# One-hots for the expert weights from one 16-bit compare, a shorter lead over U, and 18 gathered rows moved beside the last build

## The chip, the cores and the metric

The kernel runs on one core of a Trainium2 chip. A core has five engines with a queue of instructions each: TensorE (PE in the profile; its weight loads are PEld), VectorE (DVE), ScalarE (ACT), GpSimd (POOL) and SyncE (SP). They work side by side and wait for each other by semaphores; 16 DMA engines move data for all of them. The metric is the device time of one execution in microseconds (us), lower is better.

## The reference, cut to what matters

The kernel computes one encoder layer on 512 tokens of width 1024: layer norm, two kinds of attention, layer norm, then a feed-forward part that picks experts for each token, a gate, and a last layer norm. The change lies in the feed-forward part alone:

```python
q = (xb @ w_q).reshape(PEER_CHUNK, PEER_HEADS, PEER_KEY_DIM)
s1 = jnp.einsum('thd,kd->thk', q[..., :half], sub_keys[0])
s2 = jnp.einsum('thd,kd->thk', q[..., half:], sub_keys[1])
v1, i1 = lax.top_k(s1, PEER_TOPK)
v2, i2 = lax.top_k(s2, PEER_TOPK)
cand = (v1[..., :, None] + v2[..., None, :]).reshape(...)
cv, ci = lax.top_k(cand, PEER_TOPK)
e1 = jnp.take_along_axis(i1, ci // PEER_TOPK, axis=-1)
e2 = jnp.take_along_axis(i2, ci % PEER_TOPK, axis=-1)
idx = (e1 * PEER_N_KEYS + e2).reshape(...)
g = jax.nn.softmax(cv, axis=-1)
u = u_table[idx]
hpre = jnp.einsum('td,ted->te', xb, u)
act = g * jax.nn.gelu(hpre, approximate=False)
return jnp.einsum('te,ted->td', act, v_table[idx])
```

Each token has 8 heads with 16 picks, so 128 of 16,384 experts. An expert is a pair of keys (e1, e2), each 0 to 127; it has a row of U and a row of V of 1024 float32 each.

## The kernel before

**Two ways to the experts.** The 512 tokens are four chunks of 128. Chunk 0 is gathered: for each of its 128 picks an indirect DMA of POOL fetches one row of U per token (128 rows of 4 KB), and VectorE takes the dot product with the token (gather_u, L1257; the fetch is fetch_u, L1251); later the same for V (gather_v, L1266). Chunks 1 to 3 (384 tokens) are done densely: all experts are taken in 128 blocks of 128, TensorE multiplies block i of U with the tokens, ScalarE applies Gelu (the tile ge), the result is multiplied by a matrix G of weights per expert and token, and a second product adds it, times block i of V, into PSUM (acc). Of the 384, the 96 of chunk 1 with the lowest numbers take no part in the product with U; own_rows (L1002) gathers their rows of U, in 96 groups of 128 rows, and puts the result into their weights.

**G is built by TensorE.** For a token, G is the sum over its 128 picks of two one-hot vectors' product: oh_i, 1 at the first key, and oh_j, the weight at the second key. build_g (L933) takes 8 tokens (OT) at a time, 16 groups to a chunk. In a group, VectorE writes the first `first` of eight one-hots oh_i by one compare (L974), ScalarE the others by Abs and Relu (L978, L979); VectorE writes eight oh_j, one tensor_scalar each (L987: equal, then times weight). TensorE multiplies the pairs (L953, one group behind), ScalarE copies the sums out of PSUM (L964) and every second group sends 1 MB to g_dram (L966). `first` is OV_OWN = 2 for chunks 2 and 3, built first, and OV = 5 for chunk 1, built last.

**The lead.** Beside the routing of the chunks (route, L840, nearly all VectorE) and the builds, TensorE works through the gate (192 matmuls of width 512, in 16 steps of 12) and through the first LEAD = 73 blocks of U (lead_block, L1059): eight float32 matmuls of width 288 for a block, straight from the loaded block. Of these the first SPILL = 56 results go to DRAM (ge_dram) and are read back later; the others stay on the chip. A half of the gate (512 columns) ends on VectorE and ScalarE (gate_end, L1100): four loads into the tile pl, issued together on SP, and for each of the four chunks an instruction of VectorE (L1116) that reads pl. The 55 blocks left are done in the stream (expert_in, L747) as 24 matmuls each: block and tokens are split into a high and a low part, ScalarE writes the high part, VectorE the low.

**Who sets the order.** From L1191 on the order on every engine is the order in which the Python code issues. The generators yield an estimate of the VectorE time that they just issued; run (L1173) and run_pe (L924) then issue as much work of TensorE as PACE times that amount (AHEAD and LAG shift it). own_rows is woven in likewise: each yield earns it a share OWN = 0.98 of VectorE time. A row group lands in one of four buffers (whi and wlo of the pool wst, two each); its fetch waits until VectorE has read the group four before it. VectorE, ScalarE and TensorE work through their queues in order.

**The stages.** Route of chunk 1; route of chunk 2, its build, route of chunk 3, its build, with own_rows woven into these; route of chunk 0; build of chunk 1; the rest of the lead, beside which the stream is prepared (L1300 to L1318: seven row fetches of chunk 0, the load of G, loads and splits of V, seven more rows; PRE = 14 in all). Then the stream of 128 steps: each takes a block of V, 18 matmuls into acc, as long as there are any a block of U (24 matmuls), and its part of the 257 gather steps by L1366.

## Time and profile before

| | us |
|---|---|
| median of 3 runs | 1578.45 |
| the three runs | 1568.41, 1578.45, 1581.92 |
| the profiled execution | 1574.03 |
| its span, first to last instruction | 1572.2 |
| first matmul of the lead | 416.2 |
| last product of the last build | 816.6 |
| first matmul of the stream | 845.8 |

The profile is of one execution. A group line has the source line, engine, operation, tiles written <- read with their shape, the count, then the busy time of all, the mean duration of one in ns, and the engine's idle time ahead of them with what ended it. Matmuls are pipelined: their durations overlap, and a step's cost is read from the distance of starts. A float32 matmul stands as two records. A stretch line has the stretch, its length, each engine's busy time with its number of instructions, the granted TensorE clock (1.00 is full), the mean busy share of the 16 DMA engines and GB/s; the share can exceed 1 a little.

### The profile page before, as it was taken

To read this page: it belongs to the slowest core of one execution; us is meant where nothing else is said; L and a number is where in the kernel's file an instruction comes from. 1 tells how busy PE (TensorE), PEld (TensorE's weight loads), DVE (VectorE), ACT (ScalarE), POOL (GpSimd) and SP (SyncE) were. 2 spreads that over 40 slices of the span, in tenths; PEclk is the share of its full clock that TensorE was granted. 3 is DMA by queue.
4 is the path that set the end of the run, shared out by engine and by line. 5 is a ranking of instruction groups with operands and counts; after the bars stand their busy time and mean duration, and the time that the engine had idled before them with its cause. 6 is when DMAs were issued, how large, how long until landed. Compare 5 with 4: busy or idle time off the path is not lost.

```text
span 1572.2 us, 23352 instructions
## 1 busy us (share of the span) xinstructions
PE 1534.2 (98%) x7963; PEld 1275.3 (81%) x7963; DVE 1311.6 (83%) x2989; ACT 690.2 (44%) x1269; POOL 490.9 (31%) x496
## 2 busy tenths in 40 slices
PE   8999899999999999999998999999999999999997
PEld 5788777788878887888886898898998878787785
DVE  7376795679899999889985798988989898899897
ACT  3365685333224672575562334334343433333333
POOL 1013100010024233432105455555555544344410
PEclk9999999999999999999999999999999999999999
DMA  6342340152369999999769999999999999999972
GB/s 224 97 114 80 89 121 28 54 151 81 104 211 346 343 368 352 371 418 363 248 235 394 375 382 374 383 378 355 373 378 338 359 360 382 384 379 387 379 281 81
DMA packets 204571, 437.21 MB, mean 278 GB/s; under 512 B 16770, under 2 KB 110370, under 8 KB 201380
## 3 DMA queue, kind: packets, MB, share of 16 engines
q1 hardware_dynamic: 138592, 210.27, 38.9%
q0 software_dynamic: 53984, 191.97, 33.0%
q10 hardware_dynamic: 11876, 33.49, 5.5%
q8 instruction: 63, 1.03, 0.3%
q14 instruction: 56, 0.46, 0.1%
...
## 4 chain that ended last, share of the span: by engine, by line
PE 68%; DVE 12%; DMA 11%; issue 4%; ACT 2%; SPq 1%; POOL 1%; ACTq 0%; POOLq 0%; DVEq 0%
PE mm L1069 9%; DMA v_raw<-in_v_rows_dram 8%; PE acc L104 6%; PE acc L105 6%; PE acc L106 6%; PE tr L953 5%; PE hp L104 4%; PE hp L106 3%; PE hp L105 3%; PE mm L104 3%; PE mm L106 3%; PE pj L104 3%; PE mm L105 3%; PE pj L105 3%; PE pj L106 3%
## 5 line engine op out<-in xcount | busy, mean ns | idle before, releaser
L1268 POOL DMA_INDIRECT gat<-in_v_rows_dram,i_sel x128 | 170.2, 1329 | 204.8 <-DVE base L1270 180.2
L1253 POOL DMA_INDIRECT gat<-in_u_rows_dram,i_sel x128 | 170.9, 1335 | 181.7 <-DVE scr L1259 123.9
L104 PE MATMUL acc<-v_hi,a_hi 128*128 128x512 f32 x552 | 216.5, 393 | 4.0 <-ACT a_hi L89 4.0
L106 PE MATMUL acc<-v_hi,a_lo 128*128 128x512 f32 x552 | 216.2, 392 | 0.2 <-DVE a_lo L90 0.2
L105 PE MATMUL acc<-v_lo,a_hi 128*128 128x512 f32 x552 | 215.6, 391 | 0.0
L90 DVE TENSOR_TENSOR wlo<-raw,whi 128x1024 fp32r<-128x1024 f32 (+3 forms) x134 | 156.9, 1172 | 65.9 <-ACT whi L89 65.3
L89 ACT CAST whi<-raw 128x1024 fp32r<-128x1024 f32 (+3 forms) x134 | 135.1, 1009 | 139.7 <-PE mm L105 40.3
L89 ACT CAST v_hi<-v_raw 128x1024 fp32r<-128x1024 f32 x92 | 96.6, 1050 | 209.4 <-issue 121.0
L1270 DVE SCALAR_TENSOR_TENSOR base<-gat,hdot,base 128x1024 f32<-128x1024 f32 x128 | 163.8, 1280 | 1.7
L1259 DVE SCALAR_TENSOR_TENSOR scr<-gat,h 128x1024 f32<-128x1024 f32 x128 | 156.6, 1223 | 2.9
L1069 PE MATMUL mm<-whole,raw 128*128 128x288 f32 x624 | 157.2, 406 | 0.3 <-DMA raw<-in_uT_dram 0.3
L1069 PE MATMUL hp<-whole,raw 128*128 128x288 f32 x544 | 138.8, 410 | 4.2 <-DMA raw<-in_uT_dram 4.2
L89 ACT CAST a_hi<-gt 128x384 fp32r<-128x384 f32 x126 | 64.6, 513 | 177.4 <-DVE gt L1353 133.2
L1069 PEld LDWEIGHTS mm<-whole,raw 128*128 128x128 f32 x624 | 116.0, 190 | 29.9 <-DVE ci L782 0.7
L90 DVE TENSOR_TENSOR v_lo<-v_raw,v_hi 128x1024 fp32r<-128x1024 f32 x92 | 112.6, 1223 | 26.9 <-ACT v_hi L89 26.6
L104 PE MATMUL hp<-hTh,whi 128*128 128x288 f32 x440 | 130.1, 296 | 1.0 <-ACT ge L1051 1.0
L106 PE MATMUL hp<-hTh,wlo 128*128 128x288 f32 x440 | 129.9, 295 | 0.4 <-DVE wlo L90 0.4
L105 PE MATMUL hp<-hTl,whi 128*128 128x288 f32 x440 | 129.8, 295 | 0.0
L1069 PEld LDWEIGHTS hp<-whole,raw 128*128 128x128 f32 x544 | 103.2, 192 | 32.6 <-ACT v_hi L89 2.6
L104 PEld LDWEIGHTS acc<-v_hi,a_hi 128*128 128x128 f32 x552 | 103.9, 188 | 25.2 <-ACT a_hi L89 5.1
L106 PEld LDWEIGHTS acc<-v_hi,a_lo 128*128 128x128 f32 x552 | 104.0, 188 | 24.0 <-DVE a_lo L90 1.2
L105 PEld LDWEIGHTS acc<-v_lo,a_hi 128*128 128x128 f32 x552 | 104.1, 189 | 20.5 <-DVE v_lo L90 0.2
...
## 6 DMA issues: line engine op xcount, KB each, us to landing
raw<-in_uT_dram SPq DMA_DIRECT2D x128, 512.0 KB, 6.8
v_raw<-in_v_rows_dram SPq DMA_DIRECT2D x94, 512.0 KB, 10.5
...
raw<-in_v_rows_dram SPq DMA_DIRECT2D x34, 512.0 KB, 10.7
raw<-in_w_in_dram SPq DMA_DIRECT2D x16, 512.0 KB, 4.0
raw<-in_w_q_dram SPq DMA_DIRECT2D x16, 512.0 KB, 4.1
ge_dram<-ge ACTq DMA_DIRECT2D x56, 144.0 KB, 6.0
```

Source lines behind the costliest of these rows:

```text
L89: nc.scalar.copy(hi, src)
L90: nc.vector.tensor_tensor(lo, src, r32(hi), op=OP.subtract)
L104: nc.tensor.matmul(ps, a[0], b[0], start=start, stop=False)
L105: nc.tensor.matmul(ps, a[0], b[1], start=False, stop=False)
L106: nc.tensor.matmul(ps, a[1], b[0], start=False, stop=stop)
L953: nc.tensor.matmul(ps[:, i * 128:(i + 1) * 128], oj[:, 4 * r + i, :], oi[:, 4 * r + i, :], start=True, stop=True)
L1069: nc.tensor.matmul(ps[:, :N_U], raw[:, k], whole[:, k, :], start=(k == 0), stop=(k == 7))
L1253: nc.gpsimd.indirect_dma_start(out=u[:], out_offset=None, in_=u_rows, in_offset=bass.IndirectOffsetOnAxis(ap=i_sel[:, c, k:k + 1], axis=0))
L1259: nc.vector.scalar_tensor_tensor(scr, u, 1.0, h[c], op0=OP.mult, op1=OP.mult, accum_out=hdot[:, c, k:k + 1])
L1268: nc.gpsimd.indirect_dma_start(out=u[:], out_offset=None, in_=v_rows, in_offset=bass.IndirectOffsetOnAxis(ap=i_sel[:, c, k:k + 1], axis=0))
L1270: nc.vector.scalar_tensor_tensor(base[c], u, hdot[:, c, k:k + 1], base[c], op0=OP.mult, op1=OP.add)
```

## The change

- **Both keys' one-hots from one compare.** At the start of a build the two keys are also cast to fp16 (e16). In each group, VectorE compares a prepared fp16 table of 0 to 127 (iota8, each number eight times) with both keys of the eight tokens in one instruction: 2 x 128 x 8 results (m16). ScalarE copies the first half, reordered, into oh_i; of the eight oh_j, VectorE still writes the first `first` as before, and ScalarE writes the others from the second half of m16, times the weight. `first` stays 2 (OV_OWN) for chunks 2 and 3 and falls from 5 to 3 (OV) for chunk 1.
- **Shorter lead.** LEAD 73 to 63, SPILL 56 to 48. PACE 1.1 to 1.03.
- **18 rows of chunk 0 beside the last build.** The loop over gathered rows becomes a generator, rows; after own_rows it is used again for the first BESIDE = 18 row groups of chunk 0, woven into the last build. The fetches ahead of the stream start at row 18; PRE is 30, so five instead of seven rows follow them.
- **Weaving.** One share OWN becomes three: 0.6 in routes, 1.6 in builds of chunks 2 and 3, 0.65 in the last build.
- The tile pl has two buffers instead of four, and hdot is allocated earlier.

```diff
-LEAD = 73
-SPILL = 56
+LEAD = 63
+SPILL = 48
-PACE = 1.1
+PACE = 1.03
-PRE = 14
-OWN = 0.98
+BESIDE = 18
+PRE = BESIDE + 12
+OWN_R = 0.6
+OWN_B = 1.6
+OWN_G = 0.65
-OV = 5
+OV = 3
...
+    iota8 = rt.tile([128, 128, OT], F16, name="iota8")
+    nc.vector.tensor_copy(iota8, iota.unsqueeze(2).to_broadcast([128, 128, OT]))
...
-        ne = bt.tile([128, 128], F32, name="ne")
-        nc.scalar.mul(ne, ps[:, 0:128], -1.0)
+        e16 = bt.tile([128, 2, 128], F16, name="e16", bufs=1)
+        nc.vector.tensor_copy(e16, eT[:, 0:2])
+        yield 0.9
...
+            m = bt.tile([128, 2, 128, OT], F16, name="m16")
+            nc.vector.tensor_tensor(m, iota8.unsqueeze(1).to_broadcast([128, 2, 128, OT]),
+                                    e16[:, :, t0:t0 + OT].unsqueeze(2).to_broadcast([128, 2, 128, OT]), op=OP.is_equal)
             oi = bt.tile([128, OT, 128], F32, name="oh_i")
-            nc.vector.tensor_tensor(oi[:, 0:first], iota.unsqueeze(1).to_broadcast([128, first, 128]),
-                                    eT[:, 0, t0:t0 + first].unsqueeze(2).to_broadcast([128, first, 128]),
-                                    op=OP.is_equal)
-            for i in range(first, OT):
-                nc.scalar.activation(oi[:, i], iota, AF.Abs, bias=ne[:, t0 + i:t0 + i + 1])
-            nc.scalar.activation(oi[:, first:OT], oi[:, first:OT], AF.Relu, bias=1.0, scale=-1.0)
+            nc.scalar.copy(oi, m[:, 0].rearrange("p j t -> p t j"))
             if ahead:
                 sums = products(*ahead)
                 due -= 1.8
-            yield 0.15 * first
+            yield 1.2
...
-            for i in range(OT):
+            for i in range(first):
                 nc.vector.tensor_scalar(oj[:, i], iota, eT[:, 1, t0 + i:t0 + i + 1], eT[:, 2, t0 + i:t0 + i + 1],
                                         op0=OP.is_equal, op1=OP.mult)
-                if i == OT // 2 - 1:
-                    yield 0.257 * OT / 2
+            for i in range(first, OT):
+                nc.scalar.mul(oj[:, i], m[:, 1, :, i], eT[:, 2, t0 + i:t0 + i + 1])
             if ahead:
                 leave(ahead[0], sums)
             ahead = (q, oi, oj)
-            yield 0.257 * OT / 2
+            if first:
+                yield 0.257 * first
...
+    def rows(ix, x, dots, ks):
+
+        for k in ks:
+            u = wst.tile([128, D], F32, name=("whi", "wlo")[k % 2])
+            nc.gpsimd.indirect_dma_start(out=u[:], out_offset=None, in_=u_rows,
+                                         in_offset=bass.IndirectOffsetOnAxis(ap=ix[:, k:k + 1], axis=0))
+            nc.vector.scalar_tensor_tensor(u, u, 1.0, x, op0=OP.mult, op1=OP.mult, accum_out=dots[:, k:k + 1])
+            yield 1.17
...
-            pl[c] = rg.tile([128, 512], F32, name="pl", bufs=4)
+            pl[c] = rg.tile([128, 512], F32, name="pl", bufs=2)
...
-            run(route(c, res), OWN)
-            run(build_g(c, *res, OV_OWN), OWN)
+            run(route(c, res), OWN_R)
+            run(build_g(c, *res, OV_OWN), OWN_B)
...
-        run(build)
+        own = rows(i_sel[:, 0, :], h[0], hdot[:, 0, :], range(BESIDE))
+        own_due = 0.0
+        run(build, OWN_G)
+        for x in own:
+            run_pe(x)
...
-        rows = [fetch_u(0, k) for k in range(GATS - 1)]
+        some = [fetch_u(0, BESIDE + k) for k in range(GATS - 1)]
...
-        for k in range(7, PRE):
+        for k in range(BESIDE + 7, PRE):
             gather_u(0, k)
```

14 lines of the change are left out of this document (4 added, 10 removed).

## The prediction, made before the changed kernel ran

> **What bounds the kernel now.** I read the page's busy shares first, then a table by stage (the views of stretches), then prices of single instructions, then the traffic of the stages that the change touches.
>
> ```profile
> span 1572.2 us, 23352 instructions
> ...
> PE 1534.2 (98%) x7963; PEld 1275.3 (81%) x7963; DVE 1311.6 (83%) x2989; ACT 690.2 (44%) x1269; POOL 490.9 (31%) x496
> ```
>
> TensorE has something to do in 98% of the span. Only work taken from TensorE, or waits given back or added there, can move the end. The next table cuts the part that is changed at the events of the trace (first lead matmul, the three transposes ahead of each build, the last product of each build, first matmul of the stream): first route, first build, route, second build, route, last build, rest of the lead. Columns are length, busy time of each engine with counts, clock, mean busy share of the 16 DMA engines, GB/s.
>
> ```profile
> 416.20:489.40 73.20, 72.98 (x309) 57.39 (x308) 66.19 (x259) 17.37 (x29) 17.32 (x18) 1.00 0.67 218
> 489.40:594.40 105.00, 104.08 (x572) 87.50 (x571) 95.83 (x247) 72.15 (x170) 33.56 (x35) 1.00 0.98 361
> 594.40:641.80 47.40, 47.13 (x195) 36.62 (x194) 45.49 (x132) 10.37 (x20) 17.60 (x15) 1.00 0.97 355
> 641.80:730.90 89.10, 88.99 (x501) 75.38 (x500) 79.00 (x211) 64.95 (x158) 32.84 (x35) 1.00 1.01 398
> 730.90:760.80 29.90, 29.90 (x125) 23.34 (x125) 28.21 (x107) 7.04 (x13) 0.06 (x1) 1.00 0.65 233
> 760.80:816.60 55.80, 54.23 (x363) 48.25 (x362) 51.15 (x154) 42.10 (x103) 7.78 (x7) 1.00 0.73 264
> 816.60:845.80 29.20, 24.04 (x91) 17.63 (x89) 8.43 (x13) 5.56 (x9) 12.62 (x12) 0.94 0.96 348
> ```
>
> Columns after the length are PE, PEld, DVE, ACT, POOL. TensorE idles at most 1.6 us, at full clock, in any of the stages that end before 816.6. But in both first builds the DMA engines are busy without a break (0.98 and 1.01) and VectorE is at 95.83 of 105.0 and 79.00 of 89.1: three resources run out together.
>
> **TensorE's own work.** Ten blocks of U leave the lead (one pass in float32) and come back in the stream (three products of split operands).
>
> ```profile
> 739.21 21.75 PE L1069 MATMUL mm<-whole,raw 128*128 128x288 f32 x89
> ...
> 847.00 0.29 PE L104 MATMUL hp<-hTh,whi 128*128 128x288 f32 x1
> ...
> 848.20 0.30 PE L104 MATMUL hp<-hTh,whi 128*128 128x288 f32 x1
> ...
> 1400.06 0.40 PE L104 MATMUL acc<-whi,a_hi 128*128 128x512 f32 x1
> ...
> 1401.46 0.40 PE L104 MATMUL acc<-whi,a_hi 128*128 128x512 f32 x1
> ```
>
> A float32 matmul stands in the trace as two records: 21.75 / 89 x 16 records = 3.91 us a block. In the stream the matmuls start 9 apart in 1.20 us, 0.133 us each, and 24 of them make 3.20 us a block (their 0.29 us durations overlap). A 512-wide product of this kind, the gate's too, starts every 1.40 / 6 = 0.23 us. Ten blocks: -39.1 us in the lead, +32.0 us in the stream, **-7.1 us**. From the instruction orders of the two programs, the 10 blocks (80 matmuls; a two-record one is 0.489 us) leave the lead unevenly: lead matmuls by stage are 112, 97, 97, 120, 62, 51, 45 before and 96, 83, 65, 104, 55, 62, 39 after; of the 192 gate products 36 move from the first two stages into the route behind. By these, its busy time by stage becomes 61, 93, 40, 81, 26.5, 60 and 21 us.
>
> **The builds: VectorE and ScalarE.** Prices:
>
> ```profile
> L987 DVE TENSOR_SCALAR oh_j<-iota,eT 128x128 f32<-128x128 f32 x384 | 111.9, 367 | 0.0
> L974 DVE TENSOR_TENSOR oh_i<-iota,eT 128x256 f32<-128x256 f32 x32 | 13.3, 416 | 1.2 <-PE tr L953 1.1
> L974 DVE TENSOR_TENSOR oh_i<-iota,eT 128x640 f32<-128x640 f32 x16 | 13.1, 819 | 3.9 <-ACT oh_i L979 2.1 <-PE tr L953 1.4 <-ACT g_st L964 0.3
> L908 DVE TENSOR_TENSOR mask<-at_c,count_c 128x2048 f16<-128x2048 f16 x4 | 4.9, 1225 | 0.2
> L1024 DVE SCALAR_TENSOR_TENSOR whi<-whi,h_s 128x1024 f32<-128x1024 f32 x48 | 58.5, 1219 | 11.1 <-DMA whi<-in_u_rows_dram,s_sel 11.1
> L1024 DVE SCALAR_TENSOR_TENSOR wlo<-wlo,h_s 128x1024 f32<-128x1024 f32 x48 | 58.4, 1217 | 5.6 <-DMA wlo<-in_u_rows_dram,s_sel 5.4
> L978 ACT ACTIVATE oh_i<-iota,ne 128x128 f32<-128x128 f32 x240 | 75.3, 391 | 9.8 <-ACT ge L1051 2.8 <-DVE oh_j L987 2.8 <-DVE oh_i L974 2.0
> L979 ACT ACTIVATE oh_i<-oh_i 128x768 f32<-128x768 f32 x32 | 27.0, 844 | 1.0
> L979 ACT ACTIVATE oh_i<-oh_i 128x384 f32<-128x384 f32 x16 | 8.4, 523 | 0.5
> L89 ACT CAST v_hi<-v_raw 128x1024 fp32r<-128x1024 f32 x92 | 96.6, 1050 | 209.4 <-issue 121.0 <-DMA v_raw<-in_v_rows_dram 71.1 <-PE acc L106 12.5
> ```
>
> The new compare of 2048 fp16 elements has a twin in the routing: L908, is_equal on the same count, type and innermost run of 8, 1.22 us. In a build of 16 groups with OV_OWN = 2, VectorE loses 16 x 0.42 (oh_i) and 96 of 128 oh_j at 111.9 / 384 = 0.29 us, 34.6 us together, and gains 16 x 1.22 = 19.5 us: -15 us. But OWN_B = 1.6 puts 38 gathered rows into each of the first two builds where 31 stand (the orders give 10, 31, 20, 31, 4 before, 4, 38, 13, 38, 3 after), and 7 rows at 1.22 us give 9 us back. So VectorE falls to about 90 and 73 us, under TensorE's 93 and 81, by little in the first.
>
> The last build: -16 x 0.82 - 80 x 0.29 + 19.5 + 18 x 1.22 = +5.2 us, 56 us on VectorE. On ScalarE the 1024-wide copy is priced by the 1024-wide cast (1.05 us), the weighting by 75.3 / 240 = 0.31 us; 16 x 1.05 + 80 x 0.31 = 41.6 us take the place of 48 x 0.31 + 8.4 = 23.3 us: 42.1 + 18.3 = 60 us plus the issues of DMAs, against TensorE's 60. I add 3 us of waits there. Strided reads of the compare's result have no row; from below they cost nothing (nothing in a slower access can gain); from above see the rivals. ScalarE in the second build: 65.0 + 16 x (1.05 - 0.84) = 68 us, covered.
>
> **The builds: transfers.** This is the term that decides. The DMA view of the first build, the second build and the route between them, with three sizes; then one gathered row from its issue to the VectorE instruction that waits for it, then the landing times of the second build.
>
> ```profile
> DMA packets 11725, 37.89 MB, mean 361 GB/s; under 512 B 1298, under 2 KB 2842, under 8 KB 10821
> DMA packets 10324, 35.48 MB, mean 398 GB/s; under 512 B 1145, under 2 KB 3135, under 8 KB 9420
> ...
> DMA packets 5640, 16.81 MB, mean 355 GB/s; under 512 B 624, under 2 KB 2082, under 8 KB 5508
> ...
> raw<-in_uT_dram SPq DMA_DIRECT2D x128, 512.0 KB, 6.8
> ...
> ge_dram<-ge ACTq DMA_DIRECT2D x56, 144.0 KB, 6.0
> ...
> g_raw<-in_gate_w_dram SPq DMA_DIRECT2D x16, 256.0 KB, 4.1
> ```
>
> ```profile
> 657.20 0.95 POOL L1022 DMA_INDIRECT whi<-in_u_rows_dram,s_sel  x1 [0.83 <-DVE whi L1024]
> 665.69 1.22 DVE L1024 SCALAR_TENSOR_TENSOR whi<-whi,h_s 128x1024 f32<-128x1024 f32 x1 [0.53 <-DMA whi<-in_u_rows_dram,s_sel]
> DMA to landing us min/median/max: 5.8/8.3/9.7
> ```
>
> A row group is 128 x 4 KB = 0.52 MB, a U block as much, plus 0.15 MB of ge stored. Second build after: 35.48 + 7 x 0.52 - 2 blocks x 0.67 = 37.8 MB. At 398 GB/s, 95 us; TensorE needs 81. At the highest share that a long stage of this trace shows (1.05 in the next fence, so 414 GB/s), 91 us. Waits of 10 to 14 us, I take 12. First build: 37.89 + 3.67 - 1.2 - 0.4 (gate weights) = 40.0 MB; 361 GB/s gives 111 us, 398 gives 100, TensorE needs 93: 7 to 18 us. I take 10, nearer to the 398 of the stage that is full. There is a second bound: four buffers rotate, so a row can come at best every (8.3 + 1.22) / 4 = 2.4 us, 90 us for 38 rows; with the landing of 9.7 us, 104. What is queued behind a late row on VectorE is the next compare, and behind that ScalarE's copy and TensorE's products: TensorE has only the lead matmuls already ahead in its queue.
>
> Route stages: seven rows leave the second (45.5 - 8.5 + three gate splits = 38 us of VectorE beside TensorE's 40), one the third (27 beside 26.5); +2 us, since the transposes that open a build wait for the route's end. Rest of the lead: its loads are as before but seven gathers now queue on POOL behind the 18 new ones and land later; stalls there (29.2 - 24.0 us now) may grow by up to 5 us; I take 0, since five rows instead of seven follow them.
>
> **A queue on SP.** With two buffers of pl instead of four, the third and fourth load at a gate's end wait until VectorE has read the first two (L1116), and behind them on SP the next U blocks are queued, for which TensorE waits.
>
> ```profile
> 496.56 2.18 SPq L1106 DMA_DIRECT2D pl<-ple_dram  x4
> 498.84 11.89 SPq L1044 DMA_DIRECT2D raw<-in_uT_dram  x3
> ```
>
> ```profile
> L1116 DVE SCALAR_TENSOR_TENSOR mm<-mm,pl x8: 681/692/693, 512.0 to 600.8; 128x512 f32<-128x512 f32 x8
> ```
>
> So at the first gate's end the U loads move from 498.8 to behind 512.7 at the earliest, 14 us, and need 6.8 us to land. The two or three blocks loaded by then last TensorE 8 to 12 us, products and gate between them some more. At each of the two ends the cost is between 0 (the loaded blocks and the products last) and 14 + 6.8 - 11 = 10 us; a wait there overlaps those already counted in the builds, so I take 3 for both together. Less than nothing is excluded: no load comes earlier by it.
>
> **The stream.** 18 of 256 gathers and products leave it, fewer groups per step.
>
> ```profile
> 1200.00:1225.00 25.00, 25.00 (x142) 22.29 (x141) 22.46 (x24) 10.14 (x15) 12.67 (x9) 1.00 1.02 365
> 1400.00:1500.00 100.00, 99.27 (x429) 79.99 (x429) 87.89 (x105) 35.68 (x48) 41.85 (x33) 1.00 1.05 383
> ```
>
> With U beside it TensorE is full and VectorE has 2.5 of 25 us free: the ten more steps' splits fit, since L1366 spreads 227 steps over 92.5 instead of 243 over 87.5, 2.5 a step for 2.8. In the late part TensorE idles 0.7 us in 100 with transfers at 1.05; less traffic can return 2 us over the part's some 300 us.
>
> **Sum.** -7.1 + 10 + 12 (first builds) + 2 (routes) + 3 (last build) + 0 + 3 (pl) - 2 = **+21 us** on the profiled execution's 1574.0 us: 1595. That execution lies 4.4 us below the median of 1578.45 (1568.41 to 1581.92).
>
> **A rule weighed.** Beside oh_j the POOL issue of a row takes 0.95 us (657.20), and the routes, which have no oh_j, show this:
>
> ```profile
> L1022 POOL DMA_INDIRECT wlo<-in_u_rows_dram,s_sel x6: 947/1690/1691, 612.8 to 640.7; - x6
> DMA to landing us min/median/max: 4.8/7.0/8.6
> ```
>
> So issues take up to 1.69 us there, where two-tensor VectorE work follows a row, and yet land sooner (7.0 against 8.3). The Trainium skill ("SBUF — State Buffer", "Who interferes with whom") says that a tensor_scalar in a two-port mode locks GpSimd out of the ports by which descriptors are written. By that rule, taking away 96 of 128 oh_j a build would quicken the gathers; the 0.95 us row beside oh_j does not show such a lock; by the rule alone the sum would be the first rival's.
>
> **Rivals.** *TensorE stays the bound* (not slower): with the oh_j gone, rows land as in the routes, 7.0 us, a turn of (7.0 + 1.22) / 4 = 2.06 us, 38 rows in 78 us, within TensorE's need; traffic spills into the emptier routes. Over both builds and the route between, 90.2 - 1.1 = 89 MB over 214 us of TensorE work is 416 GB/s, about what share 1.05 would give. Then -7 - 2: **1565**. Against it: the share of 1.01 already there. Chance 0.30. *Landings lengthen* to 9.7 us: 104 us in the second build (+23), +18 in the first (its bound above), transition +5, routes and last build +5, less 9: 1616 at worst, **1609** at two thirds of the way there from 1595; it decides when rows in the builds turn slower than 2.4 us. Chance 0.15. *ScalarE or the compare is slow*: strided fp16 at half pace adds 16 x 1.05 + 80 x 0.16 = 30 us to the last build's ScalarE, or a compare at 2.2 us adds 16 us to VectorE in each build: **1622**. L908 speaks against the second. Chance 0.08. The forecast's own case, 1583 to 1607, has 0.47.
>
> **Numbers.** The range 1562 to 1612 holds the forecast, most of the first rival and half of the second. Runs of one kernel scatter by nearly 1%, so 1% (15.8 us, 1562.7 to 1594.2) is the bound of no change. Faster: two fifths of the first rival (1565 lies close above the bound), 0.12. Slower: half of the forecast's case and the second and third rival, 0.47. Within: 0.41.
>
> **What would show it.** Right: in the first two builds DMA share over 1, VectorE's idle time before the row products at 20 us or more (16.5 in all now), TensorE waiting for oh_j, builds of about 104 and 93 us; lead blocks 10 fewer. Wrong: builds of 94 and 81 us with no wait; landing medians near 7; or ScalarE full in the last build.

## The result, and the profile after

The changed kernel takes 1671.88 us (median of 4 runs, 1670.02 to 1672.27), the kernel before 1576.26 us on the same chip (4 runs, 1568.41 to 1581.92): a ratio of 1.0609, with a 95% interval of 1.0576 to 1.0642. It is slower by 6%, where 21 us (1.3%) were forecast, and far outside the range.

First the page's head of the changed kernel: span, then busy time, share and instructions of each engine.

```profile
span 1670.5 us, 23324 instructions
...
PE 1553.3 (93%) x8043; PEld 1288.7 (77%) x8043; DVE 1292.2 (77%) x2731; ACT 796.5 (48%) x1308; POOL 523.5 (31%) x496
```

TensorE falls from 98% to 93%, VectorE is less busy than before, ScalarE has 106 us more. ScalarE at 48% of the span does not look like a bound; the table by stage shows where it is one. The stretches are cut at the same events as in the prediction, and the columns are the same; the last row is the stream.

```profile
417.00:480.40 63.40, 61.24 (x259) 47.80 (x258) 58.18 (x245) 15.53 (x25) 9.27 (x12) 1.00 0.55 178
480.40:612.30 131.90, 101.22 (x527) 81.44 (x526) 91.83 (x175) 98.99 (x167) 58.21 (x43) 0.92 0.85 303
612.30:663.50 51.20, 41.51 (x167) 32.14 (x165) 41.48 (x114) 10.26 (x19) 12.86 (x11) 0.90 0.75 260
663.50:770.00 106.50, 87.64 (x469) 71.53 (x468) 78.95 (x156) 93.03 (x156) 51.75 (x37) 0.95 0.94 343
770.00:796.50 26.50, 26.50 (x111) 20.68 (x110) 20.31 (x75) 6.63 (x12) 3.79 (x4) 1.00 0.67 219
796.50:886.50 90.00, 70.34 (x385) 57.40 (x384) 62.97 (x115) 82.91 (x135) 21.11 (x21) 0.92 0.76 270
886.50:912.60 26.10, 21.05 (x78) 15.30 (x76) 1.81 (x3) 3.70 (x6) 9.85 (x10) 0.93 0.97 356
912.60:1670.50 757.90, 740.74 (x3864) 641.71 (x3864) 637.20 (x836) 285.39 (x399) 309.30 (x223) 0.99 0.92 332
```

The three builds take 131.9, 106.5 and 90.0 us where they took 105.0, 89.1 and 55.8. The stages from the first lead matmul to the stream last 495.6 us instead of 429.6 (+66.0), the stream 757.9 instead of 726.4 (+31.5), and 0.8 us lies ahead of them: that is the whole difference of the spans, 98.3 us. TensorE has 39.1 us less to do in the first part, so 105 us were lost there. Its idle time (length less busy time, summed over seven rows) is 86 us, 8 before: 78 us. The other 27 us are the same work done more slowly: the granted clock is 0.90 to 0.95 in most rows that hold waits, and 1.00 in the same stages before (but for the last, 0.94). Busy time times the missing share of the clock, summed over the rows, gives some 22 of the 27, an estimate; the rest is open.

What TensorE waits for stands in the groups of instructions of the whole span (busy time, mean ns of one, then idle time ahead and what ended it).

```profile
L1078 PE MATMUL hp<-whole,raw 128*128 128x288 f32 x528 | 140.2, 421 | 30.4 <-DMA raw<-in_uT_dram 30.4
L994 ACT ACTIVATE oh_j<-m,eT 128x128 f32<-128x128 f16 x272 | 118.7, 520 | 4.0 <-ACT ge L1060 3.6 <-issue 0.4
L959 PE MATMUL tr<-oh_i,oh_j 128*128 128x128 f32 x768 | 107.0, 296 | 53.0 <-ACT g_st L970 50.3 <-ACT oh_j L994 2.5
L983 ACT CAST oh_i<-m 128x1024 f32<-128x1024 f16 x48 | 100.1, 2085 | 19.7 <-DVE m L980 13.3 <-ACT ge L1060 1.6 <-ACT g_st L970 1.2
L980 DVE TENSOR_TENSOR m<-iota,e 128x2048 f16<-128x2048 f16 x48 | 58.6, 1221 | 14.9 <-ACT oh_j L994 14.5 <-issue 0.2
```

Two waits make up the idle time: 53.0 us of the products for ScalarE (mostly until it has emptied the PSUM tile that they write, L970), and 30.4 us of the lead for blocks of U. VectorE's compare costs 1.221 us as priced. ScalarE's copy costs 2.085 us, twice its price, and the weighting 520 ns where a 128-wide activation before took 391. ScalarE's timeline in the second build shows one group.

```profile
712.25 2.11 ACT L983 CAST oh_i<-m 128x1024 f32<-128x1024 f16 x1 [0.41 <-ACT g_st L970]
714.27 2.63 ACT L994 ACTIVATE oh_j<-m,eT 128x128 f32<-128x128 f16 x6
716.81 1.04 ACT L970 COPY g_st<-tr 128x512 f32<-128x512 f32 x2
...
718.55 2.06 ACT L983 CAST oh_i<-m 128x1024 f32<-128x1024 f16 x1 [0.40 <-ACT ge L1060]
```

From copy to copy 6.3 us pass, without a wait for another engine: 2.0 for the copy, 2.5 for six weightings, 1.0 for the two sums, the rest a Gelu and DMA issues. Sixteen such groups are 101 us; the second build took 106.5. The other wait is seen on SP's queue.

```profile
507.13 26.63 SPq L1115 DMA_DIRECT2D pl<-ple_dram  x4
533.81 2.20 SPq L1053 DMA_DIRECT2D raw<-in_uT_dram  x3
...
621.58 20.73 SPq L1115 DMA_DIRECT2D pl<-ple_dram  x4
```

The four loads of pl hold SP for 26.6 and 20.7 us (2.2 and 5.5 before), since the last two wait for a buffer; no block of U is issued meanwhile. TensorE's timeline has the end of the first of the two:

```profile
525.01 2.59 PE L1078 MATMUL hp<-whole,raw 128*128 128x288 f32 x10
543.26 5.14 PE L1078 MATMUL hp<-whole,raw 128*128 128x288 f32 x10 [15.67 <-DMA raw<-in_uT_dram]
```

The same ten records take 2.59 us ahead of the wait and 5.14 us behind it, which is how a wait costs TensorE more than its length.

### The profile page after: what moved, and what is told of

Read it like the earlier page. It is cut to its first block, busy times and chain, and to the rows that moved or that the text cites. A ratio compares the mean times of both kernels' runs of the same rounds, so it can differ in the third digit from the quotient of the medians.

```text
span 1670.5 us, 23324 instructions
## 1 busy us (share of the span) xinstructions
PE 1553.3 (93%) x8043; PEld 1288.7 (77%) x8043; DVE 1292.2 (77%) x2731; ACT 796.5 (48%) x1308; POOL 523.5 (31%) x496
## 3 DMA queue, kind: packets, MB, share of 16 engines
q8 instruction: 63, 1.03, 0.2%
## 4 chain that ended last, share of the span: by engine, by line
PE 67%; ACT 9%; DVE 8%; issue 7%; DMA 6%; POOL 2%; ACTq 0%; SPq 0%; POOLq 0%; DVEq 0%
PE acc L108 10%; PE acc L107 10%; PE acc L109 10%; PE hp L107 4%; PE hp L109 4%; PE hp L108 4%; ACT oh_j L994 4%; PE pj L107 3%; PE pj L108 3%; PE pj L109 3%; PE mm L107 3%; PE mm L109 3%; PE mm L108 2%; DMA wlo<-in_u_rows_dram,s_sel 2%; PE mm L1078 2%
## 5 line engine op out<-in xcount | busy, mean ns | idle before, releaser
L107 PE MATMUL acc<-v_hi,a_hi 128*128 128x512 f32 x582 | 228.4, 393 | 6.3 <-ACT a_hi L92 6.3
L109 PE MATMUL acc<-v_hi,a_lo 128*128 128x512 f32 x582 | 228.0, 393 | 0.0
L108 PE MATMUL acc<-v_lo,a_hi 128*128 128x512 f32 x582 | 227.6, 392 | 0.1
L1265 POOL DMA_INDIRECT gat<-in_u_rows_dram,i_sel x110 | 152.8, 1389 | 149.6 <-DVE scr L1271 127.5
L1078 PE MATMUL hp<-whole,raw 128*128 128x288 f32 x528 | 140.2, 421 | 30.4 <-DMA raw<-in_uT_dram 30.4
L959 PE MATMUL tr<-oh_i,oh_j 128*128 128x128 f32 x768 | 107.0, 296 | 53.0 <-ACT g_st L970 50.3
L959 PEld LDWEIGHTS tr<-oh_i,oh_j 128*128 128x128 f32 x768 | 98.1, 205 | 73.0 <-ACT g_st L970 67.9
L107 PE MATMUL hp<-hTh,whi 128*128 128x288 f32 x520 | 153.8, 296 | 0.6 <-ACT ge L1060 0.6
L109 PE MATMUL hp<-hTh,wlo 128*128 128x288 f32 x520 | 153.5, 295 | 0.4 <-DVE wlo L93 0.4
L108 PE MATMUL hp<-hTl,whi 128*128 128x288 f32 x520 | 153.4, 295 | 0.0
L1271 DVE SCALAR_TENSOR_TENSOR scr<-gat,h 128x1024 f32<-128x1024 f32 x110 | 134.5, 1223 | 2.3
```

What stands on the lines that cost most here:

```text
L107: nc.tensor.matmul(ps, a[0], b[0], start=start, stop=False)
L108: nc.tensor.matmul(ps, a[0], b[1], start=False, stop=False)
L109: nc.tensor.matmul(ps, a[1], b[0], start=False, stop=stop)
L959: nc.tensor.matmul(ps[:, i * 128:(i + 1) * 128], oj[:, 4 * r + i, :], oi[:, 4 * r + i, :], start=True, stop=True)
L1078: nc.tensor.matmul(ps[:, :N_U], raw[:, k], whole[:, k, :], start=(k == 0), stop=(k == 7))
L1265: nc.gpsimd.indirect_dma_start(out=u[:], out_offset=None, in_=u_rows, in_offset=bass.IndirectOffsetOnAxis(ap=i_sel[:, c, k:k + 1], axis=0))
```

## The experiments

Each run is set against the kernel before on the same chip; the ratio's 95% interval follows in brackets. Where two runs are compared with each other, the difference is that of their medians; the kernel before took 1574.6 to 1578.0 us (medians) beside them, so some 3 us of such a difference can come from elsewhere. In this section "lead" is the part from the first lead matmul to the first product into acc, and the stream is counted from there. What the theories were called is told in the expectations.

**1. SP's queue alone (pl_late).** The loads of pl are issued when their buffer's reader has been issued.

```diff
-        for c in range(4):
-            load(c)
+        load(0)
+        load(1)
...
             if c >= 3:
                 tasks.append(on_vector(1.2, lambda c=c: end(c - 3)))
+            if 3 <= c < 5:
+                tasks.append(lambda c=c: load(c - 1))
```

> The changed kernel, but with two buffers of pl the third and fourth load are issued only when the end that frees their buffer has been issued, so SP no longer waits ahead of the next U blocks. In the changed kernel's trace TensorE idles 15.7 + 9.7 us for U blocks behind the two pl groups, and 52.6 us for ScalarE in the builds. Theory A (ScalarE bounds the builds, SP's queue is a second and smaller loss): those 25 us go, the builds of chunks 2 and 3 stay at about 16 x 6.1 = 98 us each; 1638 to 1652. Theory B (SP's queue is the main loss and ScalarE only shows in its wake): below 1610. Theory C (the U waits lie in ScalarE's shadow and come back as waits for ScalarE): 1662 to 1672.

1651.24 us, 1.0492 (1.0471 to 1.0512): 21 us less than the changed kernel (18 by the two ratios). Its first build, the route behind it, the second and the last build:

```profile
479.70:600.00 120.30, 101.02 (x526) 81.27 (x525) 90.63 (x172) 98.56 (x166) 56.46 (x42) 0.96 0.91 330
600.00:639.70 39.70, 39.70 (x166) 31.24 (x166) 36.77 (x107) 10.43 (x19) 8.72 (x8) 1.00 0.86 296
639.70:750.00 110.30, 87.32 (x469) 70.32 (x468) 85.82 (x176) 92.97 (x156) 51.36 (x41) 0.97 0.93 346
776.50:866.40 89.90, 66.97 (x385) 54.50 (x384) 63.68 (x116) 82.85 (x135) 21.86 (x21) 0.96 0.75 269
```

The first build and the route behind it shrink from 183.1 to 160.0 us, the second build does not shrink (110.3 us for 106.5), and TensorE's waits for ScalarE are still some 57 us. Theory A: two causes, side by side.

**2. The old one-hots in the changed kernel (old_hots, and with four buffers of pl old_hots_pl4).** The diff is the change's first part backwards.

> The changed kernel with the one-hots of the kernel before (VectorE compare, Abs and Relu on ScalarE, eight weighted one-hots on VectorE, OV 5), all else as changed, the two pl buffers too. Theory A: TensorE's waits for ScalarE in the builds (52.6 us) go and the clock comes back with them, the waits for U blocks stay at about 25 us: 1595 to 1615. Theory B: the SP queue keeps it above 1630. Theory D (the weaving of more rows into the builds and the shorter lead are the main loss): above 1640.

> As the run before it, and four buffers of pl again. What is left of the change: shorter lead, the new weaving, 18 rows beside the last build. If ScalarE and SP's queue together are the whole loss, TensorE's 7.1 us less shows: 1562 to 1575. If the rows and transfers packed into the builds cost what the prediction took for them (10 + 12 + 3 us), 1585 to 1600; VectorE, at 2.4 us of one-hots for a group and 2.4 rows a group, would then be what the builds wait for.

1661.47 us, 1.0549 (1.0527 to 1.0572), and 1649.60 us, 1.0474 (1.0453 to 1.0495). Theory A missed by some 50 us; B's and D's numbers held for the first, and the second lies far above both of its bands. But the runs do not say what they were made for. The old one-hots yield 2.36 us of VectorE time a group where the new ones yield 1.71, and every yield earns OWN_B = 1.6 times its length for gathered rows: in old_hots_pl4 55 rows stood in the first build instead of the changed kernel's 42, and it took 151 us. A piece that feeds the weaving cannot be exchanged alone.

**3. The new one-hots in the kernel before (hots_only).** OV 3, loads of pl as in run 1, LEAD 71; PACE and OWN as before.

> The kernel before with the new one-hots alone (OV 3, pl loads late and LEAD 71 for the memory that they need; its own PACE and OWN, no rows beside the last build). Theory A: the builds take ScalarE's 6.1, 6.1 and 5.4 us a group, 98, 98 and 86 us where they took 105, 89 and 56: 1610 to 1630. Theory D (the lead and the weaving are the loss, the one-hots by themselves are not): below 1590.

1697.23 us, 1.0768 (1.0720 to 1.0816), worse than the whole change. The builds took 111.5, 110.2 and 92.1 us, more than the 98, 98 and 86 of theory A. The rest of the miss is the weaving again: with 1.71 us a group in place of 2.36, PACE hands TensorE less of the lead beside a build (467, 415 and 315 records in the three builds for 572, 501 and 363), and it comes later, in the route behind (52.3 us for 29.9) and after the last build (60.1 for 33.6). So the new one-hots are a loss in the old weaving too; how much of it is theirs and how much is the weaving's, this run does not part.

**4. What makes ScalarE slow (flat_reads, flat_compare, pe_strided).** All three start from pl_late. flat_reads only changes which values ScalarE reads, so its one-hots hold other values and what it computes is no longer the layer; the runs built on it (all of experiment 5, flat_lead71 and five_lead71) share this. Counts, sizes and order stay:

```diff
-            nc.scalar.copy(oi, m[:, 0].rearrange("p j t -> p t j"))
+            nc.scalar.copy(oi, m[:, 0].rearrange("p j t -> p (j t)").rearrange("p (t j) -> p t j", t=OT))
...
-                nc.scalar.mul(oj[:, i], m[:, 1, :, i], eT[:, 2, t0 + i:t0 + i + 1])
+                nc.scalar.mul(oj[:, i], m[:, 1, 16 * i:16 * i + 16, :].rearrange("p j t -> p (j t)"), eT[:, 2, t0 + i:t0 + i + 1])
```

> Base is pl_late (1651). ScalarE's copy and weightings read the same number of fp16 values from m16 but next to each other instead of 8 apart, so the one-hots hold other values; counts, sizes, waits and order stay. In pl_late TensorE idles 58 us for ScalarE in the three builds, at 2.09 us a copy and 0.42 us from one weighting to the next. Theory A (the step of 8 in the reads is what makes ScalarE the bound): copy 1.05 us, weighting about 0.3 us from start to start, the waits go, 1565 to 1598 (1592 - 3 would be the prediction's sum without SP's queue). Theory E (it is the fp16 source or the conversion, not the step): copy stays at 2.1 us, 1640 to 1655. Theory F (rows and landings packed into the builds take over at once): copy 1.05 us and yet 1605 or more, with VectorE waiting for rows.

1626.40 us, 1.0315 (1.0268 to 1.0363). The groups of instructions of flat_reads:

```profile
L994 ACT ACTIVATE oh_j<-m,eT 128x128 f32<-128x128 f16 x272 | 84.6, 390 | 4.0 <-ACT ge L1060 4.0
...
L983 ACT CAST oh_i<-m 128x1024 f32<-128x1024 f16 x48 | 50.2, 1046 | 65.0 <-DVE m L980 61.0 <-ACT g_st L970 2.4 <-ACT ge L1060 1.2
```

The copy falls from 2085 to 1046 ns and the weighting from 520 to 390: the step of 8 between the values that are read is the whole extra price; source type and conversion are the same. ScalarE now waits 61 us for the compare instead of being late. The last build gains most, 19 us:

```profile
770.20:840.70 70.50, 64.55 (x385) 54.09 (x384) 61.33 (x116) 56.99 (x135) 29.18 (x25) 0.95 0.94 350
```

The first two builds gain 7 and 5 us (113.1 and 105.4 us). The time lies above theory A's 1598: F holds, VectorE waits for rows there (more in experiment 5).

The Trainium skill ("Advanced Engine Details and Errata", section "SBUF Cachelines") says that SBUF has lines of 16 bytes, and that an access pattern with fewer than two hits on a line pays a penalty. Eight fp16 values are 16 bytes, so here each value lies in a line of its own; the trace agrees, with 2085 against 1046 ns.

flat_compare takes the step away at its source: VectorE writes token by token, with the key as a value repeated 128 times (shown in part: the table iota8 is turned round with it, and ScalarE reads in order).

```diff
-            nc.vector.tensor_tensor(m, iota8.unsqueeze(1).to_broadcast([128, 2, 128, OT]),
-                                    e16[:, :, t0:t0 + OT].unsqueeze(2).to_broadcast([128, 2, 128, OT]), op=OP.is_equal)
+            nc.vector.tensor_tensor(m, iota8.unsqueeze(1).to_broadcast([128, 2, OT, 128]),
+                                    e16[:, :, t0:t0 + OT].unsqueeze(3).to_broadcast([128, 2, OT, 128]), op=OP.is_equal)
```

> Base is pl_late. The compare itself writes token by token, each with its 128 keys in a row; the second operand is then one value repeated 128 times. ScalarE reads without steps and what is computed is the same. ScalarE as in flat_reads. If VectorE's compare of 2048 values stays at 1.22 us: as flat_reads. If the repeated operand makes it about twice as long, VectorE has 16 us more in each build and is the bound: 1605 to 1630.

1649.89 us, 1.0464 (1.0405 to 1.0524). From its groups:

```profile
L980 DVE TENSOR_TENSOR m<-iota,e 128x2048 f16<-128x2048 f16 x48 | 109.5, 2281 | 0.0
```

The compare costs 2281 ns instead of pl_late's 1220, and VectorE is the fullest engine, with 103.5 of 116.7 us in the first build: what ScalarE gains VectorE loses. The second branch, with a time 20 us above it.

pe_strided hands the step on to TensorE: oh_i stays in the compare's order.

```diff
-            oi = bt.tile([128, OT, 128], F32, name="oh_i")
-            nc.scalar.copy(oi, m[:, 0].rearrange("p j t -> p t j"))
+            oi = bt.tile([128, 128, OT], F32, name="oh_i")
+            nc.scalar.copy(oi, m[:, 0])
...
-                    nc.tensor.matmul(ps[:, i * 128:(i + 1) * 128], oj[:, 4 * r + i, :], oi[:, 4 * r + i, :],
+                    nc.tensor.matmul(ps[:, i * 128:(i + 1) * 128], oj[:, 4 * r + i, :], oi[:, :, 4 * r + i],
```

> Base is pl_late. oh_i is stored as the compare leaves it, key by key with the eight tokens inside; ScalarE copies it without reordering and TensorE reads its moving operand with a step of 8 floats; what is computed is the same. ScalarE saves 1.03 us a group, 16.5 us a build, in all three builds. If TensorE reads with a step at the same pace (0.112 us a record of a product): 1600 to 1618. If a strided operand takes it twice as long, each build has 29 us more of TensorE and the time is 1640 or more.

1667.15 us, 1.0574 (1.0524 to 1.0625). A group of products in TensorE's timeline, in pe_strided and then in the kernel before:

```profile
705.38 3.89 PE L959 MATMUL tr<-oh_i,oh_j 128*128 128x128 f32 x16
```

```profile
707.91 1.95 PE L953 MATMUL tr<-oh_i,oh_j 128*128 128x128 f32 x16
```

Sixteen records take 3.89 us instead of 1.95. All three builds became TensorE's (126.2 of 131.5, 112.1 of 114.0 and 90.4 of 90.4 us busy). In these three runs, whichever engine reads with the step pays about double, and VectorE pays it when it writes without one.

**5. The rows (flat_rows31, flat_five, flat_beside0), all from flat_reads.** VectorE's row products in the second build of flat_reads, 638.3 to 743.7:

```profile
L1011 DVE SCALAR_TENSOR_TENSOR whi<-whi,h_s 128x1024 f32<-128x1024 f32 x21 | 25.6, 1218 | 9.1 <-DMA whi<-in_u_rows_dram,s_sel 8.9
L1011 DVE SCALAR_TENSOR_TENSOR wlo<-wlo,h_s 128x1024 f32<-128x1024 f32 x21 | 25.6, 1218 | 16.5 <-DMA wlo<-in_u_rows_dram,s_sel 16.5
```

42 rows in 105.4 us, 2.51 us each, with 25 us of waits for them. What hangs behind such a wait is seen in a few lines of VectorE's timeline, and one of ScalarE's:

```profile
685.08 1.23 DVE L1011 SCALAR_TENSOR_TENSOR wlo<-wlo,h_s 128x1024 f32<-128x1024 f32 x1 [2.81 <-DMA wlo<-in_u_rows_dram,s_sel]
...
686.23 0.61 DVE L991 TENSOR_SCALAR oh_j<-iota,eT 128x128 f32<-128x128 f32 x2
...
689.63 1.05 ACT L983 CAST oh_i<-m 128x1024 f32<-128x1024 f16 x1 [3.90 <-DVE m L980]
```

Between two of its own steps of a group VectorE stands 2.8 us for a row; the next compare is queued behind, and ScalarE's next copy waits 3.9 us for it. Fewer rows:

```diff
-OWN_R = 0.6
-OWN_B = 1.6
+OWN_R = 0.98
+OWN_B = 1.28
```

> Base is flat_reads (1626), where ScalarE has 40 us free in each of the first two builds and VectorE waits 16 and 25 us for gathered rows. OWN_R 0.98 and OWN_B 1.28, so about 31 rows stand in each of these builds, as in the kernel before, and the others go back to the routes. Theory F (the turn of the four row buffers, 2.6 us a row, sets the pace of the builds): seven rows less are 15 to 18 us less in each, the routes take 5 us more each: 1598 to 1610. Theory G (TensorE is handed too little work beside the builds, whatever VectorE waits for): 1618 to 1630.

1613.57 us, 1.0254 (1.0191 to 1.0317): 13 us less than flat_reads, 4 us above theory F's band and below G's. 35 rows stood in each of the first two builds instead of 41 and 42; they took 96.1 and 92.6 us, 17 and 13 less, and the three routes 19 more. A fifth buffer:

```diff
-            u = wst.tile([128, D], F32, name=("whi", "wlo")[k % 2])
+            u = (bt.tile([128, D], F32, name="u_x", bufs=1) if k % 5 == 4 else
+                 wst.tile([128, D], F32, name=("whi", "wlo")[k % 5 % 2]))
...
-            m = bt.tile([128, 2, 128, OT], F16, name="m16")
+            m = bt.tile([128, 2, 128, OT], F16, name="m16", bufs=1)
```

> Base is flat_reads (1626). A fifth row buffer in the rotation (m16 gets one buffer instead of two for the memory). If the turn of four buffers sets the pace of the builds (2.51 to 2.83 us a row): 2.1 to 2.4 us a row, VectorE's 42 us of row waits in the first two builds fall below 15, 1600 to 1612. If the transfers are full and a fifth fetch only lengthens the landings: waits stay, 1620 to 1630.

1616.01 us, 1.0249 (1.0201 to 1.0296). Second build, 97.4 us, VectorE's row products:

```profile
L1012 DVE SCALAR_TENSOR_TENSOR wlo<-wlo,h_s 128x1024 f32<-128x1024 f32 x17 | 20.8, 1221 | 5.7 <-DMA wlo<-in_u_rows_dram,s_sel 5.7
L1012 DVE SCALAR_TENSOR_TENSOR whi<-whi,h_s 128x1024 f32<-128x1024 f32 x17 | 20.7, 1220 | 8.2 <-DMA whi<-in_u_rows_dram,s_sel 8.2
L1012 DVE SCALAR_TENSOR_TENSOR u_x<-u_x,h_s 128x1024 f32<-128x1024 f32 x9 | 11.0, 1220 | 1.4 <-DMA u_x<-in_u_rows_dram,s_sel 1.4
```

43 rows at 2.27 us. The turn of the buffers was part of it, 8 us in this build and 4 in the first; row waits about halve and do not go (15 us here, 7 in the first build). The last build grew by 5 us; the one buffer of m16 is the likely reason, not a shown one. Between the two branches, 4 us above the first one. The intervals of this run and of flat_rows31 overlap with that of flat_reads, so it is the builds' own lengths that show the gain.

flat_beside0 puts the 18 rows back into the stream (BESIDE 0, PRE 14).

> Base is flat_reads. BESIDE 0 and PRE 14: the 18 rows of chunk 0 go back into the stream. The last build took 70 us where TensorE has 60 of work. If the rows are what stretches it: 58 to 62 us for the build, and the stream, where VectorE waits for others 110 us, takes the rows at no or little cost: 1612 to 1620. If the build stays at 68 us or more, it is bound by ScalarE (57 us busy) and VectorE's chain, not by rows: 1626 to 1632.

1637.48 us, 1.0395 (1.0326 to 1.0464): 11 us more, in neither band. The last build shrinks from 70.5 to 63.6 us, so the rows did stretch it, and the stream takes them at no cost (752.3 us for 752.8). But the rows' yields had also brought lead work into the last build; without them TensorE is busy 48 of its 63.6 us, and the rest of the lead behind it takes 50 us for 31.

**6. The shorter lead (before_lead63, before63_pace, flat_lead71, five_lead71).** LEAD 63 and SPILL 48 alone in the kernel before, with PACE 1.1 and then 1.0.

> The kernel before with LEAD 63 and SPILL 48 alone. The prediction's first term by itself: 10 blocks of 3.91 us leave the lead and come back at 3.20 us, -7 us: 1564 to 1570. If the builds then wait for VectorE or transfers, since TensorE has 39 us less to put beside them, the time stays or rises: 1575 to 1600.

> The kernel before with LEAD 63 and SPILL 48 and PACE 1.0 instead of 1.1, so that lead blocks are left for the time after the last build. With PACE 1.1 (before_lead63, 1600) the blocks were used up by then and TensorE stood still for some 50 us until the first split weights came. If TensorE's work is what counts, 1574 - 7 = 1567. If the length of routes and builds is VectorE's (366 us busy of 400 and 25 of waits), the shorter lead only takes work out of the time beside it, the stages stay and the stream's 32 us come on top, less what the stages can shrink (about 10): 1588 to 1602.

1600.42 us, 1.0168 (1.0129 to 1.0207), and 1608.09 us, 1.0223 (1.0151 to 1.0295). Where -7 us was the prediction's first term, they are 26 and 33 us slower than the kernel before. The first is at the upper end of its second band, the second 6 us above it. In the first the lead ran out: after the last build TensorE had nothing for 18 us,

```profile
819.20:837.30 18.10, 0.00 (x0) 0.00 (x0) 10.07 (x15) 3.19 (x4) 8.79 (x9) 0.64 0.94 318
```

and in the stream it waited twice more for ScalarE's high part of the weighted results, the tile a_hi, 10.6 and 5.1 us: 34 us in all, where the second expectation's "some 50 us" counts the first wait twice. The second has lead left over. Here are the stretch from the first lead matmul to the end of the last build, the rest of the lead and the stream, of before63_pace and then of the kernel before:

```profile
415.60:813.50 397.90, 379.03 (x1939) 310.01 (x1939) 364.62 (x1105) 210.26 (x486) 112.17 (x109) 0.98 0.84 308
813.50:838.30 24.80, 17.54 (x72) 13.37 (x72) 11.37 (x17) 6.24 (x9) 11.63 (x12) 0.86 0.98 353
838.30:1605.80 767.50, 740.92 (x3842) 640.35 (x3840) 652.73 (x865) 282.83 (x393) 327.76 (x240) 0.98 0.94 339
```

```profile
416.20:816.60 400.40, 397.31 (x2057) 328.48 (x2056) 365.87 (x1106) 213.98 (x493) 109.17 (x109) 1.00 0.87 319
816.60:850.20 33.60, 27.77 (x115) 20.88 (x113) 12.80 (x19) 7.32 (x12) 14.10 (x14) 0.95 0.97 357
850.20:1572.20 722.00, 706.52 (x3600) 605.52 (x3600) 634.56 (x851) 269.03 (x373) 321.26 (x238) 0.99 0.96 352
```

Up to the end of the last build TensorE is busy 18 us less, and the stretch is only 2.5 us shorter: VectorE's 365 us and its waits set that length. The rest of the lead is 8.8 us shorter. So of the 39 us of work that left the lead 11 came back as time. The stream is 45 us longer, not 32; 11 us of the difference are longer waits for ScalarE's a_hi (16.8 us for 5.7). TensorE's 98% before was no proof that it alone was the bound: the lead's blocks filled whatever VectorE's pace left.

From the other side, flat_reads with eight blocks more (LEAD 71, SPILL 56, PACE 1.12), and the same with five row buffers:

> Base is flat_reads. LEAD 71 and SPILL 56, PACE 1.12: eight more blocks of U beside the routes and builds and eight fewer in the stream. By TensorE's work alone it costs 8 x (3.91 - 3.20) = 6 us: 1632. If the blocks fill time in which TensorE now waits for VectorE's rows (49 us idle in the lead, and a granted clock of 0.95 to 0.97 there), the stream gives back up to 8 x 3.20 = 26 us: 1600 to 1612.

> flat_lead71 (1608) with the fifth row buffer: ScalarE's reads without steps, SP's queue free, 71 blocks in the lead, rows in a turn of five. If these four account for the whole loss, 1572 to 1590; if something else in the change costs time, it stays above 1598.

1608.09 us, 1.0213 (1.0146 to 1.0280), the second branch: the stream is 24 us shorter and the lead only 6 us longer, though it has 31 us more work. And 1605.32 us, 1.0171 (1.0118 to 1.0223), the second branch, something else costs time too: the last build still takes 73.0 us where it took 55.8, and the stream, from which its 18 rows came, is no shorter for it (729.5 us; the kernel before has 722.0 with two blocks of U less, 6.4 us).

**7. Is there a better kernel? (products16, products16_lead81, compare16, compare16_lead81).** From the kernel before, one-hots in bfloat16, the weight as a high and a low part, two 16-bit products for a token (only the products' lines):

```diff
-                    nc.tensor.matmul(ps[:, i * 128:(i + 1) * 128], oj[:, 4 * r + i, :], oi[:, 4 * r + i, :],
-                                     start=True, stop=True)
+                    for x in range(2):
+                        nc.tensor.matmul(ps[:, i * 128:(i + 1) * 128], oj[:, x, 4 * r + i, :], oi[:, 4 * r + i, :],
+                                         start=x == 0, stop=x == 1)
```

> The kernel before, with the one-hots in bfloat16 and the weight split into a high and a low part, so each token has two 16-bit products where one float32 product stands as two records of 0.112 us. VectorE writes 16 one-hots a group instead of eight, from 16-bit tables. If a 16-bit product takes half of a record's time and a 16-bit one-hot half of 0.29 us, TensorE has some 43 us less and VectorE the same; the lead then runs out before the last build ends, as in before_lead63: 1560 to 1590. If VectorE takes as long for a 16-bit one-hot as for a float32 one, 33 us more in each build: 1630 or more.

> As products16, with LEAD 81 and SPILL 64 and a product's price of 1.0 instead of 1.8 us in the weaving, so that eight more blocks of U fill what TensorE is given back in the builds and the stream has eight fewer (26 us). If VectorE's one-hots hold their length: 1540 to 1560. If VectorE or the transfers (eight more blocks of 0.52 MB beside the builds) are the bound: 1575 or more.

1623.79 us, 1.0295 (1.0248 to 1.0342), and 1611.63 us, 1.0214 (1.0165 to 1.0263). TensorE's timeline, and groups of instructions of products16:

```profile
702.44 0.61 PE L960 MATMUL tr<-oh_i,oh_j 128*128 128x128 bf16 x8
```

```profile
L960 PE MATMUL tr<-oh_i,oh_j 128*128 128x128 bf16 x768 | 101.5, 228 | 13.6 <-DVE oh_j L995 12.2 <-ACT g_st L971 0.9 <-issue 0.3
...
L995 DVE TENSOR_SCALAR oh_j<-iota,eT 128x128 bf16<-128x128 bf16 x384 | 130.9, 347 | 0.0
L995 DVE TENSOR_SCALAR oh_j<-iota,eT,wl 128x128 bf16<-128x128 bf16 x384 | 125.9, 328 | 0.0
```

The first lies between its two bands, the second in its slower one. TensorE's part is as hoped, but 768 one-hots cost VectorE 256.8 us where 384 cost 111.9: a 16-bit one-hot of 128 elements is no cheaper than a float32 one, and VectorE is all but full in all three builds (116.2 of 117.5, 104.7 of 107.0 and 70.8 of 71.5 us). compare16 forms them all in two VectorE instructions a group, and leaves the step of 8 to TensorE (in part):

```diff
+            oi = bt.tile([128, 2, 128, OT], mybir.dt.bfloat16, name="m16")
+            nc.vector.tensor_tensor(oi, iota8.unsqueeze(1).to_broadcast([128, 2, 128, OT]),
+                                    e16[:, :, t0:t0 + OT].unsqueeze(2).to_broadcast([128, 2, 128, OT]), op=OP.is_equal)
...
+            oj = bt.tile([128, 2, 128, OT], mybir.dt.bfloat16, name="oh_j")
+            nc.vector.tensor_tensor(oj, oi[:, 1].unsqueeze(1).to_broadcast([128, 2, 128, OT]),
+                                    w16[:, :, t0:t0 + OT].unsqueeze(2).to_broadcast([128, 2, 128, OT]), op=OP.mult)
```

> The kernel before, with both keys' one-hots in bfloat16 from one compare as in the change, the weight in a high and a low part times the second half in one more VectorE instruction of 2048 values, no one-hot work on ScalarE, and TensorE reading both operands with a step of 8. VectorE: 2 x 1.22 = 2.44 us a group for 2.7 (chunks 2, 3) and 3.1 (last build). If the step costs TensorE nothing at 16 bits, 0.84 us a group for 1.67, and the lead is worked off sooner; if it doubles the time, as in pe_strided, 1.67 us as before. In both cases about as fast as the kernel before: 1560 to 1580. If the two VectorE instructions hold up POOL's issues of row fetches (0.95 us beside the tensor_scalar one-hots, up to 1.7 us beside the compare) so far that rows wait, 1590 or more.

> As compare16, with LEAD 81, SPILL 64 and a product's price of 1.0 us in the weaving: eight more blocks of U beside the builds, eight fewer in the stream. If TensorE is given back time in the builds: 1545 to 1565, faster than the kernel before. If the step doubles the products, or rows set the pace: 1575 to 1600.

1688.80 us, 1.0695 (1.0648 to 1.0741), and 1720.37 us, 1.0900 (1.0855 to 1.0946). TensorE's timeline of compare16:

```profile
706.51 3.90 PE L959 MATMUL tr<-m,oh_j 128*128 128x128 bf16 x16
```

Eight 16-bit products take 0.61 us without the step, sixteen take 3.90 with it. Taking off the last one's duration (0.228 us above; 0.413 in the groups of compare16), 0.054 and 0.233 us pass from start to start: four times as long, with the step in both operands, where the expectation had twice at most; so both times lie far beyond their bands. TensorE is full in all three builds. The granted clock is not what lengthens these products: it was 0.96 over the second build and 0.66 over the last, and sixteen of them took 3.90 us in both. No version tried beats the kernel before.

## Why the prediction was wrong, point by point

The sum fell short by 77 us (21 forecast, 98 measured). Three of its terms failed, by the runs: ScalarE's reads were taken at nothing and cost 25 us, SP's queue was taken at 3 and cost some 20, and the shorter lead was taken at -7 and cost 26 to 33 in the kernel before (with PACE 1.1 and 1.0). They overlap and cannot be added up. That the kernel came out slower, the likeliest of the three outcomes as forecast, bears out little: full transfers were to make it so, and they weren't full.

**ScalarE: the step that failed in the builds.** "Strided reads of the compare's result have no row; from below they cost nothing", and the sum took the low end: the copy at a contiguous cast's 1.05 us, a weighting at 0.31. Measured were 2.09 us and 2.5 / 6 = 0.42 from start to start. ScalarE came to 93.0 us in the second build where the prediction had 68, and to 82.9 in the last where it had 60. The third rival had the right mechanism, reads at half pace, and gave it 0.08. It priced it for the last build alone, at 30 us, and that is where most of it lay: flat_reads gives 19 us back there. In the second build too the groups ran at ScalarE's 6.3 us: the calculation of 68 us left 21 us to the build's 89, and the dear prices use that up and more (16 x (1.04 + 6 x 0.11) = 27 us). But with the cheap reads the first two builds gain only 7 and 5 us, since the waits for rows take over. flat_reads shows cause and size: 25 us of the loss, with SP's queue free.

**SP's queue: a term of the wrong size.** The prediction named the wait, what is queued behind it and who suffers, and took 3 us. pl_late shows 21; TensorE stood 15.7 and 9.7 us for U blocks, where 10 was the most that was allowed for an end. The error was to let the buffers come free when they had come free before. The first instruction that reads pl started 15.4 us behind the first load before and 23.7 us in the changed kernel (530.8), with VectorE's rows and compares ahead of it, and the four loads held SP for 26.6 and 20.7 us.

**TensorE's -7.1 us: near in the stream, not to be had in the lead.** The changed kernel's stream is 31.5 us longer; 32.0 less 2 were forecast. That is near in part by luck: in before63_pace the same ten blocks made it 45 us longer. The 39.1 us that left the lead shortened it little: by 11 us in before63_pace, and by 2.5 us up to the end of the last build. "Only work taken from TensorE ... can move the end" mistook an engine that is filled for one that bounds. The sentence behind it, "three resources run out together", was the right reading, and the sum did not follow it.

**Rows and transfers: right place, other limit.** Waits of VectorE for rows did grow, from 16.7 us (two rows of the prediction) to 37.6:

```profile
L1011 DVE SCALAR_TENSOR_TENSOR wlo<-wlo,h_s 128x1024 f32<-128x1024 f32 x47 | 57.3, 1220 | 10.4 <-DMA wlo<-in_u_rows_dram,s_sel 10.3
L1011 DVE SCALAR_TENSOR_TENSOR whi<-whi,h_s 128x1024 f32<-128x1024 f32 x47 | 57.3, 1219 | 27.2 <-DMA whi<-in_u_rows_dram,s_sel 27.2
```

But the DMA share was 0.85 and 0.94, not over 1: transfers were not full, as "DMA share over 1" demanded. The 414 GB/s of the prediction had no row of its own either: the stretch with the share of 1.05 moved 383 GB/s, less than the second build's 398 at 1.01. Even with ScalarE out of the way (flat_reads) a row took 2.51 us in the second build, not the 2.4 of the turn, and 41 or 42 rows stood there, not 38. The 22 us taken for both builds stand beside 13 and 10 us that flat_rows31 and flat_five gave back in the whole time, each alone.

**The rule weighed.** These are POOL's issues of fetches in the first two builds and the route between them, before and after:

```profile
L1022 POOL DMA_INDIRECT wlo<-in_u_rows_dram,s_sel x42 | 43.0, 1023 | 84.6 <-DVE oh_j L987 42.6 <-DVE wlo L1024 39.0 <-DVE cv L778 2.7
L1022 POOL DMA_INDIRECT whi<-in_u_rows_dram,s_sel x42 | 41.0, 977 | 72.1 <-DVE whi L1024 44.2 <-DVE oh_j L987 13.1 <-DVE cv L778 10.4
```

```profile
L1009 POOL DMA_INDIRECT whi<-in_u_rows_dram,s_sel x45 | 62.6, 1390 | 77.5 <-DVE whi L1011 51.9 <-DVE oh_j L991 10.0 <-DVE cv L784 8.5
L1009 POOL DMA_INDIRECT wlo<-in_u_rows_dram,s_sel x46 | 60.9, 1324 | 83.7 <-DVE wlo L1011 67.7 <-DVE oh_j L991 10.8 <-issue 4.9
```

An issue became longer, 1.36 us for 1.00, with three quarters of the oh_j gone. So a lock by these tensor_scalar instructions was not what slowed it, as their 0.95 us row had said. In the second build before, all issues but one took 0.95 us. In the changed kernel's second build the 18 issues that overlap a compare took 1.60 us in the mean and the other 19 took 1.20; the long ones among these lie beside a row product. In flat_compare, whose compare takes 2.28 us, the mean of all issues in these stages is 1.68 us. The same section of the Trainium skill ("SBUF — State Buffer", "Who interferes with whom") also says that a VectorE instruction with two inputs from SBUF contends with a GpSimd instruction that reads SBUF. The lengthening beside the compare and the row product, which have two, agrees with that sentence if an issue reads SBUF, which no run here takes apart.

**The rest.** VectorE's compare (1.22 us, from its twin in the routing) was right. The routes' 2 us and the last build's 3 us were lost in the waits of the first two points. Of slower work at a lower clock, up to 27 us, the prediction had nothing: the idle time in the builds came with a granted clock of 0.92 to 0.95, so a wait cost TensorE more than its length.

**What stays open.** With SP's queue free, reads without a step, five row buffers and 71 blocks in the lead the kernel is at 1605, 29 us above the kernel before. Its last build, 17 us longer with 18 rows in it, is the largest part found; its cause stays open, and taking the rows out (flat_beside0) made another kernel slower. The causes also overlap, as experiments 2 and 3 show, so the steps of this ladder (21, 25, 10 to 18) are what each gave in that order; the last step, a fifth buffer on top of 71 blocks, gave 3 us, which is not clear of the noise.
